# Hybrid trunk on one core: where the input's sums of squares and first modulation tiles are computed, and the order of w_in's blocks

## The chip, the cores and the metric

One core of a Trainium2 chip runs the whole program in one launch. The metric is the device time in microseconds, the median of several runs; a profile shows one execution of the same program. Lines (L255 and the like) are lines of the kernel before.

## The reference, cut

Two layers, 256 tokens, width 2048, all in float32. Each layer mixes the tokens by three groups of heads side by side (four retention heads, eight fox heads, four mLSTM heads), whose inputs are column blocks of one projection w_in:

```python
def reference(x, c, positions, ada_w, ada_b, norm_mix_w, norm_mlp_w, w_in, ...):
    cond = jax.nn.silu(c)
    for layer in range(DEPTH):
        mod = (cond @ ada_w[layer] + ada_b[layer])[:, None, :]
        sh_a, sc_a, g_a, sh_m, sc_m, g_m = jnp.split(mod, N_MOD, axis=-1)
        h = rmsnorm(x, norm_mix_w[layer]) * (1.0 + sc_a) + sh_a
        x = x + g_a * hybrid_mixer(h, positions, w_in[layer], ...)
        h = rmsnorm(x, norm_mlp_w[layer]) * (1.0 + sc_m) + sh_m
        x = x + g_m * (jnp.square(jax.nn.relu(h @ w_ff1[layer])) @ w_ff2[layer])
    return rmsnorm(x, final_norm_w)

def hybrid_mixer(h, ...):
    (rq, rk, rv, rg, fq, fk, fv, ff, mq, mk, mv, mo, mi, mf) = jnp.split(h @ w_in, IN_SPLIT_IDX, axis=-1)
    y_ret = head_norm(retention(rotary(rq), rotary(rk), rv)) * silu(rg)
    y_fox = head_norm(forgetting_attention(fq, fk, fv, ff + fox_f_bias))
    mq, mk = split(silu(causal_conv([mq, mk])))
    y_m = head_norm(mlstm(mq, mk, mv, mi + mlstm_i_bias, mf + mlstm_f_bias)) * sigmoid(mo)
    return (concatenate([y_ret, y_fox, y_m]) * merge_scale) @ w_out
```

## The kernel before

Activations lie transposed (features on partitions): X and the normalised h are 16 k-tiles of 128 features by 256 tokens. Every weight matrix comes in chunks of 512 KB (128x1024, two k-tiles of 512 columns) by SyncE's queue into the pool raw (6 buffers). A chunk is split in two parts for precision: ScalarE rounds it to a high part wh (L224), and VectorE or GpSimd subtracts to the low part wl (L230). Which of the two does it is set by a share per stage, pool_share: the shares are added up and at each whole one the low part goes to GpSimd. TensorE then makes three products per tile (L255 to L257 in form b for q and k blocks, L266 to L268 in form a for v, gate and output blocks), so a chunk is 24 matmuls of 256 columns or 12 of 512. wh and wl have three buffers each.

The modulation vectors are not made by matmuls: the matrix ada_w streams in 512 KB tiles through the pool ada (4 buffers), and VectorE multiplies a tile by the spread condition vector cond (in PSUM) and sums it into one column (L282). `ada_plan` lists the tiles in order, `pump` issues them at a rate per stage, and `mod_fix` folds the finished columns by three small matmuls on TensorE (L292, L293). For the first two k-tiles of layer 0, `ada_first` makes shift and scale by matmuls of one column on TensorE instead (L337), from a copy of these columns in another layout (ada_0).

At the start, ScalarE squares X, VectorE adds the squares up (L391 to L394), two fp32 matmul pairs sum over the partitions (L402) and the reciprocal root is found by Newton steps on 128x2 (`newton`), spread by `stat_spread` and used in `h_make`.

Layer 0 projects w_in in five groups of k-tiles (2, 2, 2, 4, 6), because a group can start as soon as its h is there; each group goes over the first twelve blocks of BLOCKS, and the partial sums are kept in SBUF. The last two blocks follow alone over all k-tiles ("late"). In the last group, the mixers are put to work as soon as their blocks are complete (`mixers`): they are Python generators of which `tick` advances two at a time between the matmuls, so the order of BLOCKS sets the order of retention, mLSTM and fox. Retention and mLSTM need the gate blocks rg and mo before `head_out`, which transposes the normalised heads into the operands of w_out (Y). w_out adds up four chunks kc per output block; the list `order` in `layer` names the groups behind i = 0 to 3 (0 retention, 1 and 2 fox, 3 mLSTM), and the first two output blocks begin with i = 0 and 1. Layer 1 projects all 16 k-tiles in one group, with the first block led (matmuls on X before the root is known).

A scheduler in the compiler orders the instructions of each engine by its own estimate; each engine then runs its queue strictly in that order.

Of the kernel before, what the change touches and what calls it, by code (L numbers as in the profile page):

```python
# [32 lines left out]
BLOCKS = [("rq", 0), ("rk", 512), ("rv", 1024), ("mq", 5128), ("mk", 5640), ("mv", 6152), ("fq0", 2048), ("fk0", 3072),  # L33
          ("fv0", 4096), ("fq1", 2560), ("fk1", 3584), ("fv1", 4608), ("rg", 1536), ("mo", 6664)]
# [13 lines left out]
            pool_win=[1.0, 1.0, 1.0, 1.0, 0.5], pool_late=0.5, pool_out=0.3, pool_ff1=[0.3, 0.8], pool_ff=0.8),  # L48
# [14 lines left out]
class Trunk:  # L63
# [52 lines left out]
    def constants(self):  # L116
# [8 lines left out]
        self.ccol = c.tile([P, KT], F32, name="ccol")  # L125
        nc.sync.dma_start(self.ccol, io["ccol"])
# [9 lines left out]
        nc.scalar.activation(self.ccol, self.ccol, AF.Silu)  # L136
# [134 lines left out]
    def ada(self, l, j, kt):  # L271
# [55 lines left out]
    def ada_first(self, kts):  # L327

        nc = self.nc
        ps = self.bank((P, 512))  # L330
        n = len(kts)
        for i in range(2 * n):
            for h in range(2):
                raw = (self.raw if h else self.adap).tile([P, 8, P], F32, tag="raw" if h else "ada", name=self.name("raw"))
                nc.sync.dma_start(raw, self.io["ada_0"][:, i, 8 * h:8 * h + 8, :])
                for k in range(8):
                    nc.tensor.matmul(ps[:, i:i + 1], lhsT=raw[:, k, :], rhs=self.ccol[:, 8 * h + k:8 * h + k + 1],  # L337
                                     start=i == 0 and h == 0 and k == 0, stop=False, skip_group_check=True)
        for i, j in enumerate((1, 0)):
            s = slice(i * n, i * n + n)  # L340
            nc.tensor.matmul(ps[:, s], lhsT=self.ident, rhs=self.vcol(0, C_ADAB + j * KT + kts[0], n), start=False,
                             stop=True, skip_group_check=True)
        a = self.mod[0]
        nc.vector.scalar_tensor_tensor(a[:, KT + kts[0]:KT + kts[0] + n], ps[:, 0:n], 1.0,
                                       self.vcol(0, C_NMIX + kts[0], n), ALU.add, ALU.mult)
        nc.scalar.copy(a[:, kts[0]:kts[0] + n], ps[:, n:2 * n])
# [684 lines left out]
    def run(self):  # L1031
# [11 lines left out]
        for q in range(4):  # L1043
            self.stat_piece(q)
# [115 lines left out]
```

## Time and profile before

| | us |
|---|---|
| median of 3 runs | 2580.16 (2579.64 to 2580.45) |
| profiled execution | 2578.99 |
| its span, first to last instruction | 2577.0 |
| TensorE busy in the span | 2468.7 (96%) |
| VectorE busy | 1576.0 (61%) |
| ScalarE busy | 1183.5 (46%) |
| GpSimd busy | 732.8 (28%) |

Busy shares are averages over stages with different limits; a busy TensorE may run at the lower of its two clock levels (1.2 and 2.4 GHz), which the column PEclk shows as a share of the higher. Windows are counted from the first instruction.

### The profile page before, as it was taken

What the parts mean: (1) busy time and instruction counts of PE and PEld (TensorE: products, weight loads), DVE (VectorE), ACT (ScalarE), POOL (GpSimd) and SP (SyncE); (2) the same over time, 40 slices, a digit from 0 to 9 for tenths busy, and PEclk for the clock granted to TensorE, in tenths of its full rate; (3) what the DMA queues carried; (4) which work ended last, traced back from release to release, by engine and by line L of the source; (5) the groups of instructions that cost most, each with busy time, mean ns of one, the idle gap of its engine ahead of it and who ended that gap; (6) DMA issues with size and microseconds to landing.
All of it is one profiled execution on the core that took longest, in us unless ns stands there. A gap on an engine that the chain in (4) does not pass through costs nothing.

```text
span 2577.0 us, 46671 instructions
## 1 busy us (share of the span) xinstructions
PE 2468.7 (96%) x19116; PEld 2394.2 (93%) x19116; DVE 1576.0 (61%) x2429; ACT 1183.5 (46%) x1445; POOL 732.8 (28%) x303
## 2 busy tenths in 40 slices
PE   7999998798999999999999899999999999999997
PEld 6899886698999999999998889989999999999997
DVE  3676986589665444444468877656755555554555
ACT  2544453545553444443445454554644444444443
POOL 1786431122576766666661000000000000000000
PEclk9999998899999999999999999999999999999999
DMA  7899876398998887888877677645555555555552
GB/s 276 283 342 327 291 270 224 138 352 318 357 333 319 295 285 277 298 290 288 284 254 255 219 275 269 218 145 180 173 185 184 188 180 188 184 185 183 185 186 101
DMA packets 177390, 630.45 MB, mean 245 GB/s; under 512 B 19732, under 2 KB 24470, under 8 KB 177176
## 3 DMA queue, kind: packets, MB, share of 16 engines
q1 hardware_dynamic: 176744, 627.09, 70.0%
q8 instruction: 149, 2.44, 0.4%
q14 instruction: 65, 0.53, 0.1%
q10 hardware_dynamic: 432, 0.39, 0.1%
HBM read 625.31 MB, written 2.10 MB: 243 GB/s over the span
## 4 chain that ended last, share of the span: by engine, by line
PE 80%; DVE 9%; DMA 3%; issue 3%; POOL 3%; ACT 2%; SPq 0%; DVEq 0%; POOLq 0%; ACTq 0%
PE pj L255 22%; PE pj L256 22%; PE pj L257 22%; PE pj L267 3%; POOL wl L230 3%; PE pj L266 3%; PE pj L268 3%; DVE ada L282 2%; DVE wl L230 2%; DMA ada<-ada_w 2%; PE mx L337 1%; PE mx L625 1%; DMA raw<-w_in 1%; DVE cv L714 1%; ACT wh L224 0%
## 5 line engine op out<-in xcount | busy, mean ns | idle before, releaser
L224 ACT CAST wh<-raw 128x1024 fp32r<-128x1024 f32 x804 | 840.6, 1047 | 1108.6 <-PE pj L257 902.9
L230 DVE TENSOR_TENSOR wl<-raw,wh 128x1024 fp32r<-128x1024 f32 x506 | 622.7, 1232 | 488.4 <-ACT wh L224 487.8
L230 POOL TENSOR_TENSOR wl<-raw,wh 128x1024 fp32r<-128x1024 f32 (+1 forms) x298 | 730.2, 2453 | 635.8 <-ACT wh L224 559.2
L256 PE MATMUL pj<-hh,wl 128*128 128x256 f32 x2912 | 829.9, 285 | 16.6 <-DVE wl L230 16.6
L255 PE MATMUL pj<-hl,wh 128*128 128x256 f32 x2912 | 830.4, 285 | 2.2 <-DVE hl L505 1.4
L257 PE MATMUL pj<-hh,wh 128*128 128x256 f32 x2912 | 828.1, 284 | 0.0
L255 PE MATMUL pj<-blk,wh 128*128 128x256 f32 x2528 | 716.1, 284 | 5.4 <-ACT blk L543 3.0
L256 PE MATMUL pj<-blk,wl 128*128 128x256 f32 x2528 | 715.3, 283 | 5.0 <-DVE wl L230 4.0
L257 PE MATMUL pj<-blk,wh 128*128 128x256 f32 x2528 | 712.7, 282 | 0.0
L282 DVE SCALAR_TENSOR_TENSOR ada<-ada,cond 128x1024 f32<-128x1024 f32 x376 | 453.4, 1215 | 260.5 <-DMA ada<-ada_w 257.8
L256 PEld LDWEIGHTS pj<-hh,wl 128*128 128x128 f32 x2912 | 561.2, 193 | 19.0 <-DVE wl L230 18.2
L255 PEld LDWEIGHTS pj<-hl,wh 128*128 128x128 f32 x2912 | 560.9, 193 | 4.0 <-DVE hl L505 1.9
L257 PEld LDWEIGHTS pj<-hh,wh 128*128 128x128 f32 x2912 | 561.0, 193 | 0.2
L256 PEld LDWEIGHTS pj<-blk,wl 128*128 128x128 f32 x2528 | 481.6, 190 | 5.7 <-DVE wl L230 4.4
L255 PEld LDWEIGHTS pj<-blk,wh 128*128 128x128 f32 x2528 | 480.6, 190 | 6.5 <-ACT blk L543 3.5
L257 PEld LDWEIGHTS pj<-blk,wh 128*128 128x128 f32 x2528 | 480.9, 190 | 0.0
L1054 POOL TENSOR_TENSOR blk<-blk,R 128x1024 f32<-128x1024 f32 x1 | 2.4, 2355 | 1201.8 <-ACT R L424 1201.8
L801 DVE SCALAR_TENSOR_TENSOR X<-pj,mod,X 128x256 f32<-128x256 f32 x284 | 117.8, 477 | 67.4 <-PE pj L257 67.4
L267 PE MATMUL pj<-wl,hh 128*128 128x512 f32 x384 | 152.6, 397 | 3.5 <-DVE wl L230 3.0
L266 PE MATMUL pj<-wh,hl 128*128 128x512 f32 x384 | 151.9, 396 | 0.0
L268 PE MATMUL pj<-wh,hh 128*128 128x512 f32 x384 | 151.0, 393 | 0.0
L267 PEld LDWEIGHTS pj<-wl,hh 128*128 128x128 f32 x384 | 72.3, 188 | 19.4 <-DVE wl L230 5.2
(232 smaller groups left out, 1663.6 us busy)
## 6 DMA issues: line engine op xcount, KB each, us to landing
raw<-w_ff SPq DMA_DIRECT2D x508, 512.0 KB, 4.0
ada<-ada_w SPq DMA_DIRECT2D x376, 512.0 KB, 6.4
raw<-w_in SPq DMA_DIRECT2D x224, 512.0 KB, 5.2
raw<-w_out SPq DMA_DIRECT2D x64, 512.0 KB, 4.5
raw<-ada SPq DMA_DIRECT2D x8, 512.0 KB, 8.7
X<-x SPq DMA_DIRECT2D x4, 512.0 KB, 6.1
raw<-w_ff SPq DMA_DIRECT2D x8, 256.0 KB, 3.5
out<-blk SPq DMA_DIRECT2D x4, 512.0 KB, 2.8
```

What stands on the lines that cost most here:

```text
L224: nc.scalar.copy(hi, raw)
L230: eng.tensor_tensor(lo, raw, hi.bitcast(F32), ALU.subtract)
L255: nc.tensor.matmul(o, lhsT=wh[:, s], rhs=al, start=st, stop=False, skip_group_check=True)
L256: nc.tensor.matmul(o, lhsT=wl[:, s], rhs=ah, start=False, stop=False, skip_group_check=True)
L257: nc.tensor.matmul(o, lhsT=wh[:, s], rhs=ah, start=False, stop=last, skip_group_check=True)
L266: nc.tensor.matmul(o, lhsT=al[:, s], rhs=wh, start=first, stop=False)
L267: nc.tensor.matmul(o, lhsT=ah[:, s], rhs=wl, start=False, stop=False)
L268: nc.tensor.matmul(o, lhsT=ah[:, s], rhs=wh, start=False, stop=last)
L282: nc.vector.scalar_tensor_tensor(raw, raw, 1.0, self.cond, ALU.mult, ALU.mult, accum_out=self.part[l][:, i, h:h + 1])
L337: nc.tensor.matmul(ps[:, i:i + 1], lhsT=raw[:, k, :], rhs=self.ccol[:, 8 * h + k:8 * h + k + 1], start=i == 0 and h == 0 and k == 0, stop= ...
L625: nc.tensor.matmul(ps[:, i * P:i * P + P], lhsT=lt, rhs=v[:, j, c:c + P], start=first, stop=last, skip_group_check=True)
L801: V.scalar_tensor_tensor(self.X(k), ps[:, n * T:n * T + T], self.mod[l][:, c:c + 1], self.X(k), ALU.mult, ALU.add)
```

## The change

The input's sums of squares: `stat_first` lets TensorE multiply the squares by a matrix of ones, 16 fp32 matmuls of 256 columns that add up over the partitions and leave the sum on every partition, so nothing has to be spread; the Newton steps then run on 128x256. The first modulation tiles: `ada_first` and its arrays ada_0 and ccol are gone, the k-tiles 0 and 1 are the first of the plan, and `pump_until` puts their eight tiles on VectorE; the first four of them use buffers of raw. The blocks of w_in: fox first, then mLSTM, then retention, then the gates mo and rg; w_out takes the groups in the order fox, fox, mLSTM, retention. In the last group of layer 0, GpSimd's share of low parts is 0.8 instead of 0.5. The fork of buffers in `newton` makes room in SBUF for the 128x256 tiles.

VectorE at the start, where the reciprocal root and the first modulation tiles are made (nw are Newton's tiles, ada and raw modulation tiles, part their sums). Before:

```order
L375 TENSOR_TENSOR nw_154<-mx_147,nw_154 128x2
L376 SCALAR_TENSOR_TENSOR nw_155<-nw_154,mx_147 128x2
L497 TENSOR_TENSOR mx_258<-X_91,R 128x512
L282 SCALAR_TENSOR_TENSOR ada_351,part_127<-ada_351,cond 128x1024
L282 SCALAR_TENSOR_TENSOR ada_354,part_127<-ada_354,cond 128x1024
```

After:

```order
L355 TENSOR_TENSOR nw_156<-mx_128,nw_155 128x256
L298 SCALAR_TENSOR_TENSOR mod_126<-mx_188,vec 128x2
L283 SCALAR_TENSOR_TENSOR ada_196,part_124<-ada_196,cond 128x1024
L356 TENSOR_TENSOR nw_156<-mx_128,nw_156 128x256
L357 SCALAR_TENSOR_TENSOR mx_128<-nw_156,mx_128 128x256
L355 TENSOR_TENSOR nw_156<-mx_128,nw_155 128x256
L356 TENSOR_TENSOR nw_156<-mx_128,nw_156 128x256
L357 SCALAR_TENSOR_TENSOR mx_128<-nw_156,mx_128 128x256
L355 TENSOR_TENSOR nw_156<-mx_128,nw_155 128x256
L356 TENSOR_TENSOR nw_156<-mx_128,nw_156 128x256
L357 SCALAR_TENSOR_TENSOR nw_157<-nw_156,mx_128 128x256
L492 TENSOR_TENSOR mx_204<-X_91,nw_157 128x512
```

The eight modulation products now stand among the first Newton steps; eight steps of 128x256 follow the last of them (ada_196).

TensorE around group 0 of w_in (pj_450 is its seventh block before, pj_577 its twelfth after; mx_945 and mx_891 are the same mod_fix, for the scale of k-tiles 4 and 5). Before:

```order
L256 MATMUL pj_450<-hh,wl_454 128x256
L257 MATMUL pj_450<-hh,wh_453 128x256
L292 MATMUL mx_945<-part_127,fold 128x2 x2
L293 MATMUL mx_945<-vec,ident 128x2
L255 MATMUL pj_489<-hl,wh_492 128x256
```

After:

```order
L265 MATMUL pj_577<-wh_580,hh 128x512
L293 MATMUL mx_891<-part_124,fold 128x2
L252 MATMUL pj_641<-hl,wh_644 128x256
L293 MATMUL mx_891<-part_124,fold 128x2
L294 MATMUL mx_891<-vec,ident 128x2
L253 MATMUL pj_641<-hh,wl_645 128x256
```

The step moved from the seventh block of group 0 to the first of group 1; the one behind it (the shift) moved from the tenth block of group 0 to behind the second of group 1.

TensorE at the end of the projections of layer 0 (before: pj_4067 is the last gate block, mx_3578 to mx_3684 are fox heads; after: pj_4300 and pj_4454 are w_out's first two output blocks, mx_3969 to mx_4076 retention heads, mx_4125 an output transposition of mLSTM). Before:

```order
L267 MATMUL pj_4067<-wl_4320,hh 128x512
L268 MATMUL pj_4067<-wh_4319,hh 128x512
L665 MATMUL mx_3578<-ident,pt_3587 128x128 x3
L625 MATMUL mx_3578<-blk_546,pt_3587 128x128 x3
L652 MATMUL mx_3684<-blk_520,blk_481 128x128
```

After:

```order
L254 MATMUL pj_4300<-blk_3619,wh_4378 128x256
L620 MATMUL mx_3860<-blk_596,pt_3863 128x128 x3
L609 MATMUL mx_3969<-blk_531,blk_575 128x256
L610 MATMUL mx_3969<-blk_531,blk_575 128x128
L620 MATMUL mx_3969<-blk_596,pt_3972 128x128 x3
L609 MATMUL mx_4015<-blk_531,blk_575 128x256
L610 MATMUL mx_4015<-blk_531,blk_575 128x128
L620 MATMUL mx_4015<-blk_596,pt_4018 128x128 x3
```

Five fox heads stood behind the projections' last matmul and ahead of w_out; now the last three retention heads stand behind w_out's first block, and the mLSTM transposition ahead of its second.

The diff, with the removed function and the loader of its arrays cut:

```diff
-BLOCKS = [("rq", 0), ("rk", 512), ("rv", 1024), ("mq", 5128), ("mk", 5640), ("mv", 6152), ("fq0", 2048), ("fk0", 3072),
-          ("fv0", 4096), ("fq1", 2560), ("fk1", 3584), ("fv1", 4608), ("rg", 1536), ("mo", 6664)]
+BLOCKS = [("fq0", 2048), ("fk0", 3072), ("fv0", 4096), ("fq1", 2560), ("fk1", 3584), ("fv1", 4608),
+          ("mq", 5128), ("mk", 5640), ("mv", 6152), ("rq", 0), ("rk", 512), ("rv", 1024), ("mo", 6664), ("rg", 1536)]
...
-            pool_win=[1.0, 1.0, 1.0, 1.0, 0.5], pool_late=0.5, pool_out=0.3, pool_ff1=[0.3, 0.8], pool_ff=0.8),
+            pool_win=[1.0, 1.0, 1.0, 1.0, 0.8], pool_late=0.5, pool_out=0.3, pool_ff1=[0.3, 0.8], pool_ff=0.8),
...
-        self.ccol = c.tile([P, KT], F32, name="ccol")
-        nc.sync.dma_start(self.ccol, io["ccol"])
...
-        nc.scalar.activation(self.ccol, self.ccol, AF.Silu)
...
-                raw = self.adap.tile([P, n], F32, tag="ada", name=self.name("ada"))
+                early = self.nada < 4
+                self.nada += 1
+                raw = (self.raw.tile([P, n], F32, tag="raw", name=self.name("raw")) if early else
+                       self.adap.tile([P, n], F32, tag="ada", name=self.name("ada")))
...
-    def ada_first(self, kts):
...
+        mk = lambda nm: self.small.tile(list(shape), F32, tag=f"nw{nm}{shape[-1]}", name=self.name("nw"),
+                                          bufs=1 if shape[-1] == T else 2)
...
+    def stat_first(self):
+        nc = self.nc
+        ps = self.bank((P, 512))
+        for q in range(4):
+            sq = self.slot()
+            nc.scalar.activation(sq, self.Xq[q], AF.Square)
+            for i in range(4):
+                nc.tensor.matmul(ps[:, :T], lhsT=self.ones, rhs=sq[:, i, :], start=q == 0 and i == 0,
+                                 stop=q == 3 and i == 3)
+        v = self.small.tile([P, T], F32, name="nv0", bufs=1)
+        nc.vector.tensor_scalar(v, ps[:, :T], 1.0 / D, EPS, ALU.mult, ALU.add)
+        self.R = self.newton(v, (P, T), ps[:, T:2 * T])
...
-        order = [1, 2, 0, 3]
+        order = [1, 2, 3, 0]
...
-        for k in range(2, KT, 2):
+        for k in range(0, KT, 2):
             self.ada_plan([(0, (1, 0), [k, k + 1])])
...
-        self.stat_begin()
-        for q in range(4):
-            self.stat_piece(q)
-        self.stat_end()
-        self.ada_first([0, 1])
-        self.h_make(0, 0, 1, [0, 1], True)
+        self.stat_first()
+        self.pump_until(0, 0, 1)
```

## Rows read from the trace of the kernel before

**Rows 1.** The page, bandwidth in 40 slices of 64.4 us

```profile
GB/s 276 283 342 327 291 270 224 138 352 318 357 333 319 295 285 277 298 290 288 284 254 255 219 275 269 218 145 180 173 185 184 188 180 188 184 185 183 185 186 101
```

**Rows 2.** Stretches of layer 0: busy us (instructions) per engine, granted clock, DMA

```profile
core 0: us, PE busy (x) PEld busy (x) DVE busy (x) ACT busy (x) POOL busy (x), PEclk, DMA share, GB/s
80.00:100.00 20.00, 14.49 (x86) 13.51 (x85) 17.49 (x26) 8.98 (x14) 9.66 (x4) 0.83 0.74 246
100.00:240.00 140.00, 140.00 (x1009) 132.57 (x1008) 101.65 (x135) 60.23 (x72) 112.96 (x47) 1.00 0.94 336
260.00:340.00 80.00, 73.96 (x492) 67.44 (x491) 79.82 (x112) 38.15 (x46) 39.08 (x13) 0.98 0.84 297
423.00:457.00 34.00, 21.58 (x88) 14.94 (x87) 20.38 (x72) 15.20 (x46) 0.00 (x0) 0.64 0.26 99
457.00:500.00 43.00, 29.97 (x203) 27.27 (x204) 21.43 (x61) 23.54 (x46) 4.79 (x2) 0.81 0.21 71
500.00:560.00 60.00, 60.00 (x511) 60.00 (x510) 51.69 (x83) 25.84 (x31) 14.42 (x7) 1.00 0.99 372
```

**Rows 3.** Order of time at the start: start us, duration us, instruction

```profile
4.52 3.78 PE L139 MATMUL cond<-crow,csel 2*128 2x512 f32 x4 [4.52 <-ACT crow L137]
19.25 27.30 PE L337 MATMUL mx<-ccol,raw 128*128 128x1 f32 x128
26.37 1.22 DVE L282 SCALAR_TENSOR_TENSOR ada<-ada,cond 128x1024 f32<-128x1024 f32 x1 [5.77 <-DMA ada<-ada_w]
55.39 0.70 DVE L497 TENSOR_TENSOR mx<-X,R 128x512 f32<-128x512 f32 x1
56.12 0.56 PE L255 MATMUL pj<-hl,wh 128*128 128x256 f32 x1
58.81 0.69 DVE L505 TENSOR_TENSOR hl<-mx,hh 128x512 fp32r<-128x512 f32 x1
60.32 0.41 PE L256 MATMUL pj<-hh,wl 128*128 128x256 f32 x1
60.81 0.28 PE L256 MATMUL pj<-hh,wl 128*128 128x256 f32 x1
```

**Rows 4.** The loads of line 335: issue durations, first and last issue, landing

```profile
L335 SPq DMA_DIRECT2D raw<-ada x8: 328/455/571, 4.5 to 10.9; - x8
DMA to landing us min/median/max: 7.5/8.7/10.2
```

**Rows 5.** Order of time, 80 to 91 us: VectorE, GpSimd and TensorE

```profile
80.24 2.59 DVE L187 TENSOR_SCALAR rt<-rt,rope 128x256 f32<-128x256 f32 x1
80.28 2.40 POOL L230 TENSOR_TENSOR wl<-raw,wh 128x1024 fp32r<-128x1024 f32 x1 [0.43 <-ACT wh L224]
90.54 0.38 PE L292 MATMUL mx<-part,fold 128*128 128x2 f32 x2 [3.18 <-DVE ada L282]
```

**Rows 6.** Groups and single lines, 250 to 424 us (min/median/max ns, or mean ns)

```profile
L230 DVE TENSOR_TENSOR wl<-raw,wh 128x1024 fp32r<-128x1024 f32 x26 | 31.6, 1214 | 5.4 <-ACT wh L224 5.3
L694 DVE TENSOR_TENSOR pt<-mx,decay 128x256 f32<-128x256 f32 x4 | 1.7, 419 | 0.0
L714 DVE SCALAR_TENSOR_TENSOR cv<-blk,vec,cv x24: 460/466/2605, 292.6 to 344.7; 128x255 f32<-128x255 f32 x8, 128x254 f32<-128x254 f32 x8, 128x253 f32<-128x253 f32 x8
L230 POOL TENSOR_TENSOR wl<-raw,wh x26: 2374/2413/5291, 248.6 to 415.6; 128x1024 fp32r<-128x1024 f32 x26
```

**Rows 7.** What TensorE waited for, 423 to 500 us, and its order of time

```profile
PE mx L786 <- ACT blk L771: 11.8, 6, 9.8
471.02 0.94 PE L625 MATMUL mx<-blk,pt 128*128 128x128 f32 x6 [0.21 <-DVE pt L666]
482.86 0.48 PE L786 MATMUL mx<-ident,blk 128*128 128x128 f32 x1 [9.78 <-ACT blk L771]
```

**Rows 8.** Stretches of layer 1, columns as in rows 2

```profile
1420.00:1440.00 20.00, 11.81 (x76) 10.80 (x75) 18.81 (x29) 9.32 (x10) 0.00 (x0) 0.82 0.61 204
1720.00:1740.00 20.00, 16.61 (x110) 15.29 (x110) 7.92 (x18) 11.46 (x20) 0.00 (x0) 0.83 0.30 106
```

More of the change, by code (lines that the diff above doesn't have):

```diff
@@ L325, in flush @@
                 self.h_make(0, 0, 1, kts, True)
-    def ada_first(self, kts):
[L329 to L346, printed above, removed]
     def rate(self, tiles, units):
@@ L365, in newton @@
         n = int(np.prod(shape[1:]))
-        mk = lambda nm: self.small.tile(list(shape), F32, tag=f"nw{nm}{shape[-1]}", name=self.name("nw"))
+        mk = lambda nm: self.small.tile(list(shape), F32, tag=f"nw{nm}{shape[-1]}", name=self.name("nw"),
+                                          bufs=1 if shape[-1] == T else 2)
         y = ps[:, :n] if len(shape) == 2 else ps[:, :n].rearrange("p (a b) -> p a b", b=shape[2])
@@ L1032, in run @@
         nc = self.nc
-        self.pending, self.credit, self.out_tiles, self.U, self.wdma, self.fixes = [], 0.0, [], {}, [], []
-        for k in range(2, KT, 2):
+        self.pending, self.credit, self.out_tiles, self.U, self.wdma, self.fixes, self.nada = [], 0.0, [], {}, [], [], 0
+        for k in range(0, KT, 2):
             self.ada_plan([(0, (1, 0), [k, k + 1])])
@@ L1084, in _layout @@
     a["positions"] = np.ascontiguousarray(inp["positions"][0])
-    a["ccol"] = np.ascontiguousarray(inp["c"].reshape(KT, P).T)
-    w0 = inp["ada_w"][0].reshape(KT, P, 6, KT, P)[:, :, 1::-1, 0:2, :]
-    a["ada_0"] = np.ascontiguousarray(w0.transpose(1, 2, 3, 0, 4)).reshape(P, 4, KT, P)
     a["ada_w"] = np.ascontiguousarray(inp["ada_w"].transpose(0, 2, 1)).reshape(DEPTH, 96, 2, P, D // 2)
```

## The prediction

> **What bounds the kernel now.** I read the bandwidth line of the page first, then a table of stretches (busy time, granted clock, load traffic), then the order of time in the two places where TensorE stands still, and last the VectorE and GpSimd groups of the last w_in group. The projections need TensorE: from 100 to 240 us it is busy 140.00 of 140 us [rows 2]. So a microsecond counts only where TensorE waits or runs at the lower level of its clock. What a stretch loses I take as its length less busy time times granted clock [rows 2]: 80 to 100 us loses 20 - 14.49 x 0.83 = 8.0; 260 to 340 loses 80 - 73.96 x 0.98 = 7.5; 423 to 457 loses 34 - 21.58 x 0.64 = 20.2; 457 to 500 loses 43 - 29.97 x 0.81 = 18.7. In layer 1 the same sum gives 10.3 for 1420 to 1440 and 6.2 for 1720 to 1740 [rows 8]. Ahead of all that, the first projection matmul starts at 56.12 us [rows 3].
>
> **The start.** TensorE makes the first modulation columns itself: 128 one-column matmuls take 27.30 us from 19.25 on [rows 3]. The change removes them, the two spread matmuls and the VectorE sums, and puts 16 fp32 matmuls of 256 columns (sums of squares) on TensorE and eight 128x1024 products on VectorE. The loads are the same in number and size (8 x 512 KB). The pieces:
> - Sums on TensorE: the two 512-column fp32 matmuls of cond take 3.78 us from 4.52 on [rows 3], so one of 256 columns costs 0.95 us at that pace and 0.47 at the doubled pace that matmuls show at 60.81, after TensorE had run since 56.12 without a break (0.41 recorded at 60.32, 0.28 at 60.81) [rows 3]. From 8.3 on, 16 of them end at 15.9 or at 23.4. I take 15.9, since TensorE has work without a break from 4.52.
> - Tiles: the eight loads are issued from 4.5 to 10.9 and land 7.5 to 10.2 us later, so the last is there by about 20 [rows 4]; its product is 1.22 [rows 3]: 21.3.
> - Newton on 128x256 is 13 steps; a VectorE step of that size with a PSUM operand takes 0.419 us [rows 6]. Eight of them stand behind the last product: 3.4, so 24.7. From the multiplication by R to the stored low part is 55.39 to 59.50 = 4.1 us [rows 3]: the first projection matmul at 29. With the sums at 23.4, four products (4.9), 12 steps (5.0) and the 4.1 follow: 37.4. **Term: 56.1 to 29, minus 27 (bounds minus 19 and minus 28).**
>
> **80 to 100 us.** The rope steps on VectorE stand ahead of a modulation product, and TensorE waits 3.18 us for that at 90.54; a rope step of 128x256 takes 2.59 us there, ending with a GpSimd low part that ran beside it [rows 5]. In the new order the mod_fix steps for k-tiles 4 and 5 stand behind group 0 and two blocks into group 1, where before they stood inside group 0. **Term: minus 8, if the products come in time.** They come from the load stream, though: by 240 us it has moved 64.4 x (0.276 + 0.283 + 0.342) + 46.8 x 0.327 = 73.3 MB [rows 1]. The same point would now be due at 240 - 27 - 8 = 205. Ten tiles (5.2 MB) can be ahead of their use, so 68 MB are due by 205, 337 GB/s from the first load on; 100 to 240 us showed 336 with a DMA share of 0.94, and 500 to 560 showed 372 [rows 2]. There is no slack. I take 6 us back (bounds 0 and 20).
>
> **Last w_in group of layer 0 (pool_win 0.5 to 0.8).** 36 chunks: 11 low parts go from VectorE to GpSimd, 11 x 1.214 = 13.4 us less VectorE [rows 6]. VectorE was the bound from 260 to 340 (79.82 of 80) [rows 2]; with fox first, the rotary multiplications leave this place too. Against it: a GpSimd low part has a median of 2.41 us but takes up to 5.29, and the convolution's 24 steps have a median of 0.47 but take up to 2.61 [rows 6]: the two engines hold each other. All 24 held for the longest would be 24 x 2.14 = 51 us; I take four more than now, 9 us, since GpSimd's parts grow from 18 to 29. **Term: minus 4 of the 7.5 lost (bounds minus 7 and plus 12).**
>
> **End of the projections, layer 0.** Before, w_out starts with the fox outputs, which are the last to be computed. TensorE waits 11.8 us for the normalised heads [rows 7]; from the last value product of fox 1 (471.02) to its first output transposition (482.86) it is 11.8 us, 9.78 of it idle [rows 7]. Now fox is done early and w_out's first two blocks cover the rest. What stays: three retention heads in a row behind the projections (scores, two VectorE steps, values), some 2.8 us each with 1.3 of work: 4.5 lost; the mlstm heads' transpositions in front of the second w_out block, with a chain of 11.8 plus its gate (1.2 and the sigmoid's column) less the 9 us of the heads: 5; then the retention's own 13 to 14 us behind some 8 us of matmuls: 5; and 2 at the lower clock. Together 16 of the 38.9. **Term: minus 23 (bounds minus 32 and minus 5).**
>
> **Layer 1.** No group, share or load changes; only the order. Retention's start (rotary on VectorE and ScalarE) meets the gates at 1420, which costs the 10.3; fox's tail costs the 6.2. Fox has no 128x1024 steps at its start, and retention now has two whole blocks behind it. New collisions when the rotary starts beside pool_win 0: 5 of the 16.5 come back. **Term: minus 11 (bounds minus 16 and plus 3).**
>
> **Given back later.** Part of w_out's modulation products and low parts lay in the 77 us in which TensorE was half idle, and now has to run beside full matmuls; from 500 to 560 VectorE is busy 51.69 of 60 and DMA 0.99 [rows 2]. **Term: plus 4 (bounds 0 and plus 15).** The edits to newton's buffers and the w_out order cost nothing by themselves: their price is inside the terms above.
>
> Sum: -27 - 8 + 6 - 4 - 23 - 11 + 4 = -63. The profiled execution takes 2578.99 us (span 2577.0 and 2.0 around it), so 2516; the median of the three runs is 1.2 higher, so **2517 us**.
>
> **Rivals.** (1) *The load stream and VectorE take the gains of layer 0 back.* All layer-0 traffic (to 560 us) is then moved at a pace near what the rows show as an average: the early start and the tail bring the same loads due earlier, and both engines that feed TensorE are at 0.85 to 0.99. Then 20 us are lost up to 240 and 15 in w_out instead of 6 and 4: -38, so **2542**. For it: 336 GB/s with TensorE full. Against it: 372 in 500 to 560, so more is possible. The Trainium skill (SBUF — State Buffer, A bandwidth-pool intuition that's wrong) puts one core's HBM traffic at about 358 GB/s; the 372 of the trace is above that, and the measurement decides. (2) *The tail only changes its name*: mlstm and retention end as late as fox did, because both share two PSUM banks and VectorE with w_out. Then the term is minus 3, and the sum -43: **2537**. (3) *Nothing is given back*: loads and VectorE keep up, the tail loses 8: -27 - 8 - 7 - 31 - 15 = -88, so **2492**. (4) *Slower: GpSimd's low parts become the bound.* A block's chunk takes TensorE some 2.85 us; a low part that VectorE holds takes 5.29 [rows 6]. If all 29 GpSimd parts of the last group take that, TensorE waits 29 x 2.44 = 71 us there, more than the 63 + 4 gained: **2584**. It turns slower from a mean of 5.2 us per part. Against it: the median of 26 is 2.413, so only a few are held, and eleven fewer VectorE low parts hold them. The Trainium skill (SBUF — State Buffer, Who interferes with whom) has it that a VectorE instruction with two SBUF inputs and a GpSimd instruction that reads SBUF shut each other out for a whole instruction; the rope step of 2.59 and the 5.29 agree, and by that rule this case would need every low part to meet such an instruction.
>
> **How the numbers follow.** Forecast as summed 0.46, (1) 0.19, (2) 0.15, (3) 0.16, (4) 0.03, and 0.01 for no difference. The range has to hold eight in ten: the forecast and both middle rivals are in it, with their unknown bounds up to 2555 and, toward (3), down to 2490: **2490 to 2555**. Slower by over 0.2% (about 5 us, what a measurement of this kernel can tell from no change) 0.03, within 0.01, faster 0.96.
>
> **What would show it.** The first projection matmul near 29 us, not 37; no TensorE wait of 3 us on a modulation product before 100; over 330 GB/s up to 210 us; no fox transposition waited for at the end of the projections, but one short wait each for mlstm and retention heads, 16 us lost together; TensorE full where 1420 was, less the time gained. It would be wrong if the first group waits for w_in loads behind the modulation loads, if TensorE waits for GpSimd low parts in the last w_in group, or if w_out of layer 0 waits for weights, which it did not from 500 to 560 [rows 2].

## The result and the profile after

The changed kernel takes **2547.36 us** (median of 4 runs, 2546.65 to 2549.75), against 2579.9 for the kernel before beside it: ratio 0.9877, 95% interval 0.9860 to 0.9894, so 32.5 us faster. The forecast was 2517 with a range of 2490 to 2555: inside the range, with about half of the gain that was summed up. The profiled execution took 2549.75 us (span 2548.0), 29.2 less than the one before. One of the ten runs of the kernel called e8 below took 5384.98 us for no known reason; its median is 2574.05 with it and 2573.85 without. Lines are now those of the changed kernel; L252 to L254, L227, L283 and L293 are what L255 to L257, L230, L282 and L292 were.

The page: busy times, and the bandwidth in 40 slices, to be held against [rows 1].

```profile
PE 2450.1 (96%) x19016; PEld 2378.3 (93%) x19016; DVE 1583.2 (62%) x2427; ACT 1180.9 (46%) x1442; POOL 758.9 (30%) x314
GB/s 359 299 327 329 305 217 265 285 299 338 322 334 310 279 288 297 287 280 298 285 213 241 272 247 266 192 166 178 178 182 186 188 182 183 187 185 183 186 187 91
```

Stretches of the changed kernel (length, busy us of each engine with its instructions, granted clock, DMA share, GB/s), answering to [rows 2] and [rows 8]:

```profile
core 0: us, PE busy (x) PEld busy (x) DVE busy (x) ACT busy (x) POOL busy (x), PEclk, DMA share, GB/s
20.00:40.00 20.00, 11.15 (x61) 10.80 (x62) 14.19 (x27) 7.12 (x10) 8.57 (x4) 0.59 1.02 378
60.00:80.00 20.00, 14.72 (x89) 13.56 (x88) 19.53 (x28) 7.86 (x9) 11.99 (x5) 0.85 0.77 275
100.00:220.00 120.00, 120.00 (x860) 113.38 (x859) 86.33 (x114) 48.78 (x57) 96.36 (x42) 1.00 0.94 332
240.00:320.00 80.00, 80.00 (x572) 74.47 (x571) 70.60 (x136) 37.07 (x62) 47.58 (x20) 1.00 0.87 311
320.00:400.00 80.00, 72.64 (x398) 60.39 (x397) 57.33 (x121) 45.76 (x78) 30.06 (x13) 0.98 0.68 233
400.00:460.00 60.00, 48.24 (x292) 43.00 (x291) 50.36 (x123) 30.05 (x54) 8.78 (x4) 0.83 0.55 199
460.00:520.00 60.00, 60.00 (x511) 60.00 (x510) 48.85 (x78) 26.41 (x32) 14.21 (x7) 1.00 0.96 360
520.00:600.00 80.00, 64.03 (x465) 62.65 (x464) 73.32 (x122) 37.80 (x61) 12.79 (x6) 0.87 0.81 284
1300.00:1360.00 60.00, 49.21 (x352) 48.18 (x352) 42.19 (x69) 31.24 (x53) 21.27 (x9) 0.86 0.58 200
```

Length less busy time times clock, as in the prediction: 60 to 80 us still loses 7.5; 240 to 320 loses nothing (260 to 340 of the kernel before, with VectorE full, lost 7.5); 320 to 400 loses 8.8; 400 to 460 loses 20.0; 520 to 600 loses 24.3; and 1300 to 1360, the joint between the layers, loses 17.7.

What a stretch loses says little where two kernels do different work in it. A second reading does: every variant computes the same projections, so I add up the columns of the pj matmuls in the trace and note when the n-th chunk's worth (6144 columns) is done. Layer 0 has 60 chunks in groups 0 to 3, the last group up to 96, the gate blocks up to 112, w_out up to 144; layer 1 begins at 393. The table gives that time less the time of the kernel before, in us; a step from one row to the next is what the stretch between them won or lost. All columns behind "changed" are the experiments told below (e1, e2, e3, e8, e6, e9, e10 and e12, from left to right); each rests on one execution.

| chunks done | before, at us | changed | start only | order only | share 0.5 | start and share | joint mended | both mends | mends, old start | rope at start |
|---|---|---|---|---|---|---|---|---|---|---|
| 0 | 56.7 | -24.6 | -24.2 | 0.0 | -24.6 | -24.6 | -24.1 | -24.4 | 0.2 | -23.2 |
| 16 | 113.1 | -22.2 | -21.3 | -0.2 | -22.9 | -21.9 | -22.4 | -30.7 | -7.7 | -31.1 |
| 40 | 185.2 | -23.4 | -22.5 | -0.2 | -24.1 | -23.1 | -23.6 | -31.7 | -7.0 | -31.7 |
| 64 | 261.7 | -21.5 | -20.6 | -0.2 | -22.2 | -21.2 | -21.7 | -21.0 | -1.8 | -29.9 |
| 120 | 507.2 | -41.2 | -15.5 | -7.0 | -39.8 | -12.7 | -41.8 | -39.0 | -11.9 | -48.4 |
| 160 | 651.7 | -34.2 | -19.9 | -10.7 | -32.7 | -13.3 | -34.7 | -37.2 | -6.9 | -50.9 |
| 396 | 1329.2 | -33.9 | -20.4 | -11.8 | -33.0 | -13.1 | -31.0 | -35.2 | -4.3 | -48.3 |
| 420 | 1428.9 | -24.5 | -20.2 | -12.7 | -26.7 | -5.3 | -29.4 | -33.7 | -1.1 | -46.6 |
| 516 | 1757.3 | -32.1 | -19.7 | -22.0 | -39.1 | -6.2 | -38.9 | -43.9 | -10.7 | -55.3 |

So the changed kernel's 29.2 us are made up of: start -24.6, groups 0 to 3 +3.1, last group and tail of layer 0 -19.7, w_out and the start of ff1 +7.0, the rest up to chunk 516 +2.1, and +2.9 behind it.

One execution is not exact, and two pairs of columns show by how much. Up to 1290 us, TensorE and VectorE run the same instructions in the same order in the changed kernel and in e6 ("joint mended"); yet e6 is 0.5 us ahead of the changed kernel at chunk 320 and 2.9 behind it at chunk 340, since from 1080 to 1120 us its TensorE is busy 38.27 of 40 us at a granted clock of 0.96, against 40.00 at 1.00. From 1337 us on, the same holds for the changed kernel and e3 ("share 0.5"); yet between chunks 420 and 516 e3 wins 12.4 us and the changed kernel 7.6. So a step of the table can be off by 3 to 5 us.

**The start**, in order of time (start, duration, instruction, idle before):

```profile
7.75 9.53 PE L415 MATMUL mx<-blk,ones 128*128 128x256 f32 x32
22.34 1.21 DVE L283 SCALAR_TENSOR_TENSOR ada<-ada,cond 128x1024 f32<-128x1024 f32 x1
26.69 0.42 DVE L357 SCALAR_TENSOR_TENSOR nw<-nw,mx 128x256 f32<-128x256 f32 x1
31.46 0.58 PE L252 MATMUL pj<-hl,wh 128*128 128x256 f32 x1 [6.84 <-DVE hl L500]
```

**The rope steps**, which make the tables of the rotary embedding, still stand ahead of modulation products, only earlier. 64 to 76 us, VectorE, GpSimd and TensorE:

```profile
65.83 2.44 DVE L196 TENSOR_SCALAR rt<-rt 128x256 f32<-128x256 f32 x1
68.60 2.36 POOL L227 TENSOR_TENSOR wl<-raw,wh 128x1024 fp32r<-128x1024 f32 x1 [0.48 <-ACT wh L221]
68.64 2.59 DVE L201 SCALAR_TENSOR_TENSOR rt<-rt 128x256 f32<-128x256 f32 x1
71.16 1.21 DVE L283 SCALAR_TENSOR_TENSOR ada<-ada,cond 128x1024 f32<-128x1024 f32 x1
72.43 0.38 PE L293 MATMUL mx<-part,fold 128*128 128x2 f32 x2 [3.16 <-DVE ada L283]
```

TensorE waits 3.16 us here, 2.12 once more at 75.16, and then runs at the lower level: the same loss as the wait of 3.18 in [rows 5], moved with the work.

**The joint of the layers**, 1312 to 1323 us:

```profile
1312.30 1.22 DVE L283 SCALAR_TENSOR_TENSOR ada<-ada,cond 128x1024 f32<-128x1024 f32 x1 [1.31 <-DMA ada<-ada_w]
1312.48 7.69 POOL L227 TENSOR_TENSOR wl<-raw,wh 128x1024 fp32r<-128x1024 f32 x3 [1.79 <-ACT wh L221]
1313.44 2.00 DVE L374 TENSOR_TENSOR ss<-ss,blk 128x512 f32<-128x512 f32 x1
1315.36 5.48 DVE L437 SCALAR_TENSOR_TENSOR blk<-X,mod,blk 128x256 fp32r<-128x256 f32 x3
1323.04 1.87 PE L383 MATMUL pj<-ones,ss 128*128 128x1 f32 x8 [6.12 <-DVE ss L375]
```

A modulation product waits 1.31 us for its load, the steps behind it (sum of squares L374, operands of the lead block L437) then run beside three GpSimd low parts, and take 2.0 us, and 5.48 for three, instead of the 0.68 and 0.42 each that they take in e6 below, without those parts. TensorE waits 6.12 us for the second sum of squares (L375) at 1323.04. In the kernel before, both sums stand ahead of that product, and TensorE doesn't wait for them:

```profile
1344.25 0.69 DVE L393 TENSOR_TENSOR ss<-ss,blk 128x512 f32<-128x512 f32 x1
1345.39 0.69 DVE L394 TENSOR_TENSOR ss<-ss,blk 128x512 f32<-128x512 f32 x1
1349.00 1.22 DVE L282 SCALAR_TENSOR_TENSOR ada<-ada,cond 128x1024 f32<-128x1024 f32 x1 [2.13 <-DMA ada<-ada_w]
```

### The profile page after: what moved, and what is told of

The parts are those of the page before. It is cut to its first block, busy times and chain, and to the rows that moved or that the text cites. A ratio compares the mean times of both kernels' runs of the same rounds, so it can differ in the third digit from the quotient of the medians.

```text
span 2548.0 us, 46455 instructions
## 1 busy us (share of the span) xinstructions
PE 2450.1 (96%) x19016; PEld 2378.3 (93%) x19016; DVE 1583.2 (62%) x2427; ACT 1180.9 (46%) x1442; POOL 758.9 (30%) x314
## 3 DMA queue, kind: packets, MB, share of 16 engines
q8 instruction: 149, 2.44, 0.4%
## 4 chain that ended last, share of the span: by engine, by line
PE 79%; DVE 9%; DMA 4%; issue 3%; POOL 3%; ACT 2%; SPq 0%; DVEq 0%; POOLq 0%; ACTq 0%
PE pj L253 23%; PE pj L252 23%; PE pj L254 23%; DMA ada<-ada_w 3%; POOL wl L227 3%; DVE ada L283 2%; PE pj L264 2%; PE pj L265 2%; PE pj L263 2%; DVE wl L227 2%; PE mx L620 1%; ACT wh L221 1%; DVE cv L709 1%; DVE blk L437 0%; DMA raw<-ada_w 0%
## 5 line engine op out<-in xcount | busy, mean ns | idle before, releaser
L227 POOL TENSOR_TENSOR wl<-raw,wh 128x1024 fp32r<-128x1024 f32 (+1 forms) x309 | 756.3, 2451 | 583.4 <-ACT wh L221 565.3
L227 DVE TENSOR_TENSOR wl<-raw,wh 128x1024 fp32r<-128x1024 f32 x495 | 615.7, 1246 | 487.4 <-ACT wh L221 486.7
L252 PE MATMUL pj<-hl,wh 128*128 128x256 f32 x2912 | 830.9, 286 | 9.5 <-DVE hl L500 8.2
L254 PE MATMUL pj<-hh,wh 128*128 128x256 f32 x2912 | 828.1, 284 | 0.0
L252 PE MATMUL pj<-blk,wh 128*128 128x256 f32 x2528 | 712.8, 282 | 2.8 <-ACT blk L538 1.5
L254 PE MATMUL pj<-blk,wh 128*128 128x256 f32 x2528 | 711.3, 281 | 0.0
L283 DVE SCALAR_TENSOR_TENSOR ada<-ada,cond 128x1024 f32<-128x1024 f32 x380 | 456.7, 1214 | 227.7 <-DMA ada<-ada_w 225.6
L252 PEld LDWEIGHTS pj<-hl,wh 128*128 128x128 f32 x2912 | 561.8, 193 | 10.7 <-DVE hl L500 8.9
L254 PEld LDWEIGHTS pj<-hh,wh 128*128 128x128 f32 x2912 | 562.1, 193 | 0.2
L252 PEld LDWEIGHTS pj<-blk,wh 128*128 128x128 f32 x2528 | 478.8, 190 | 3.4 <-ACT blk L538 1.9
L254 PEld LDWEIGHTS pj<-blk,wh 128*128 128x128 f32 x2528 | 479.3, 190 | 0.0
L264 PEld LDWEIGHTS pj<-wl,hh 128*128 128x128 f32 x384 | 73.7, 192 | 24.5 <-DVE wl L227 10.7
```

The source lines that it names most:

```text
L227: eng.tensor_tensor(lo, raw, hi.bitcast(F32), ALU.subtract)
L252: nc.tensor.matmul(o, lhsT=wh[:, s], rhs=al, start=st, stop=False, skip_group_check=True)
L254: nc.tensor.matmul(o, lhsT=wh[:, s], rhs=ah, start=False, stop=last, skip_group_check=True)
L264: nc.tensor.matmul(o, lhsT=ah[:, s], rhs=wl, start=False, stop=False)
L283: nc.vector.scalar_tensor_tensor(raw, raw, 1.0, self.cond, ALU.mult, ALU.mult, accum_out=self.part[l][:, i, h:h + 1])
```

## The experiments

Medians; a ratio is to the kernel before on the same chip in the same sitting. In the five sittings the kernel before took 2576.57 to 2579.9 us, so a difference of medians from two sittings can be off by 2 to 3 us.

| kernel | us | ratio (95% interval) |
|---|---|---|
| changed | 2547.36 | 0.9877 (0.9860 to 0.9894) |
| e1 start only | 2567.65 | 0.9957 (0.9942 to 0.9972) |
| e2 order only | 2557.82 | 0.9928 (0.9909 to 0.9947) |
| e3 changed, share 0.5 | 2547.80 | 0.9882 (0.9864 to 0.9901) |
| e4 changed, layer 1 in the old order | 2552.94 | 0.9909 (0.9892 to 0.9925) |
| e5 changed, constants behind group 2 | 2537.80 | 0.9843 (0.9822 to 0.9864) |
| e6 changed, joint without GpSimd | 2540.03 | 0.9843 (0.9823 to 0.9864) |
| e7 changed, rotary of layer 1 on GpSimd | 2547.46 | 0.9874 (0.9853 to 0.9896) |
| e8 start and share, old order | 2574.05 | 0.9983 (0.9973 to 0.9992) |
| e9 joint mended, constants inside group 3 | 2538.91 | 0.9853 (0.9838 to 0.9867) |
| e10 as e9, old start | 2568.84 | 0.9963 (0.9951 to 0.9975) |
| e11 as e9, w_out share 0.6 | 2539.97 | 0.9855 (0.9840 to 0.9871) |
| **e12 joint mended, rope tables at the start** | **2522.95** | **0.9784 (0.9767 to 0.9801)** |

### The parts alone: e1 and e2

e1 keeps the changed kernel's start and takes back the rest (e2 is the other half: BLOCKS and the w_out order in the kernel before).

```diff
-BLOCKS = [("fq0", 2048), ("fk0", 3072), ("fv0", 4096), ...
+BLOCKS = [("rq", 0), ("rk", 512), ("rv", 1024), ("mq", 5128), ...
-            pool_win=[1.0, 1.0, 1.0, 1.0, 0.8], ...
+            pool_win=[1.0, 1.0, 1.0, 1.0, 0.5], ...
-        order = [1, 2, 3, 0]
+        order = [1, 2, 0, 3]
```

(Lines of e4 and e12 are shifted by one to five against the changed kernel's.)

> The start alone: sums of squares on TensorE and the first modulation tiles on VectorE; blocks, w_out order and share as before. Theory (what the two traces show by matmuls done): the first projection matmul comes 24.6 us earlier, some 3 us of it go to the rope steps, and nothing later takes it back: 2580 - 21 = 2559 us. Rival (the load stream, due earlier, takes part of it back up to the end of layer 0's projections): 2580 - 11 = 2569 us.

> The order alone: w_in's blocks fox, mlstm, retention, mo, rg and w_out's order; old start, share 0.5. Theory: the last w_in group and the tail of layer 0 gain some 20, w_out gives 7 back, layer 1 gives 2 back: 2580 - 11 = 2569 us. Rival (the tail only changes its name, mlstm and retention end as late as fox did): 2580 - 3 = 2577 us.

Measured: the start alone 10.4 us in the median, the order alone 20.2; together 30.6, close to the changed kernel's 32.5. Going from e2 to e3, which differ by the start alone, is 10.0 as well. But the profiled execution of e1 (2559.27) was the quickest of its six (the others 2564.56 to 2569.92), and in its trace the start's 24 us are still 19.7 at chunk 516. So the rival's number was met and its reason not shown: up to chunk 64 nothing but 3.6 us is taken back, and where the other executions lose some 5 to 10 us more, no trace here tells. The order alone gave more than the theory's 11, because layer 1 gains 10.2 with it (-11.8 at chunk 396 to -22.0 at 516): the forecast of -11 for layer 1 fits a kernel whose joint is clean.

### The share: e3 and e8

```diff
-            pool_win=[1.0, 1.0, 1.0, 1.0, 0.8], pool_late=0.5, ...
+            pool_win=[1.0, 1.0, 1.0, 1.0, 0.5], pool_late=0.5, ...
```

That is e3; e8 is e1 with the share left at 0.8.

> The changed kernel with GpSimd's share of 0.5 instead of 0.8 in the last w_in group of layer 0. Theory: eleven low parts return to VectorE (13 us of its time), which is full from 400 to 420 us only, so some 4 us are lost: 2551 us. Rival (the share is worth nothing, or GpSimd holds VectorE): 2543 to 2547 us.

> The changed kernel in the old order of blocks and of w_out: the start and the share 0.8 alone. Theory: with the start alone 10 us are won in the median (2567.65); in the old order VectorE is full from 260 to 340 us, so eleven low parts fewer on it are worth the 7 us lost there: 2561 us. Rival (the share only moves the wait, GpSimd parts being held as long as VectorE's were short): 2567 us.

Both theories fell. In the new order the share is worth nothing (2547.80 and 2547.36); in the old order it costs 6.4 us (2567.65 to 2574.05), 7 us above the rival's 2567. Where these 6.4 go is not shown: e8's trace loses 7.9 us between chunks 64 and 160 where e1's loses 0.7, but also 7.8 at the joint, where e1's loses 0.2. GpSimd itself is not what is late. In the changed kernel its 36 low parts of 230 to 417 us (minimum, median, maximum in ns) are

```profile
L227 POOL TENSOR_TENSOR wl<-raw,wh x36: 2373/2403/3352, 230.7 to 404.5; 128x1024 fp32r<-128x1024 f32 x36
```

against a maximum of 5291 in [rows 6]. e8 also shows that the tail's reading was right: in the old order the fox transposition of [rows 7] is waited for as before, and not in any kernel with the new one.

```profile
471.23 0.47 PE L781 MATMUL mx<-ident,blk 128*128 128x128 f32 x1 [9.83 <-ACT blk L766]
```

### Layer 1: e4 and e7

```diff
+OLD_ORDER = [9, 10, 11, 6, 7, 8, 0, 1, 2, 3, 4, 5, 13, 12]
...
+        if l == 1:
+            b = OLD_ORDER[b]
...
-        order = [1, 2, 3, 0]
+        order = [1, 2, 3, 0] if l == 0 else [1, 2, 0, 3]
```

> The changed kernel with layer 1 alone in the old order (blocks retention, mlstm, fox, rg, mo and w_out retention third). Theory: the new order only exchanges one stall of layer 1 for another, since the rotary of retention meets VectorE low parts wherever it stands: 2545 us, 2 less than the changed kernel, with 10 us lost at the gates again. Rival (the forecast): the order is worth 11 us in layer 1, and something else took them: 2558 us.

Measured 2552.94: neither 2545 nor 2558. The new order is worth 5.6 us in layer 1. With the old one TensorE waits at the gates as it did before (7.7 us there):

```profile
1413.92 0.58 PE L254 MATMUL pj<-hh,wl 128*128 128x256 f32 x1 [8.19 <-DVE wl L228]
```

In the new order the rotary steps of retention meet the low parts later, and for less: VectorE of the changed kernel at 1646, and TensorE's wait.

```profile
1646.28 1.22 DVE L682 TENSOR_TENSOR blk<-blk,blk 128x1024 f32<-128x1024 f32 x1
1647.41 2.35 DVE L227 TENSOR_TENSOR wl<-raw,wh 128x1024 fp32r<-128x1024 f32 x2
1648.69 0.80 PE L264 MATMUL pj<-wl,hh 128*128 128x512 f32 x1 [3.23 <-DVE wl L227]
```

e7 moves these rotary steps to GpSimd, which has no other work in layer 1 behind its first blocks:

```diff
-            V.tensor_tensor(x, x, cb, ALU.mult)
-            V.tensor_tensor(sw, sw, sb, ALU.mult)
-            V.tensor_tensor(x, x, sw, ALU.add)
+            E = nc.gpsimd if l == 1 else V
+            E.tensor_tensor(x, x, cb, ALU.mult)
+            E.tensor_tensor(sw, sw, sb, ALU.mult)
+            E.tensor_tensor(x, x, sw, ALU.add)
```

> The changed kernel with the rotary products of layer 1 on GpSimd, which has nothing else to do there. Theory: at 1641 to 1648 us six 128x1024 rotary steps stand ahead of VectorE's low parts, and TensorE waits 3.2 us and runs at the lower level behind it, 6.9 lost; that is gone: 2541 us. Rival (GpSimd's steps hold VectorE's low parts one by one, as they do in layer 0): 2547 us.

Measured 2547.46, no gain: the rival. Four low parts on VectorE take 12.66 us beside GpSimd's rotary, 3.2 each instead of 1.22, and TensorE waits 2.17 us in place of 3.23:

```profile
1636.38 2.40 POOL L681 TENSOR_TENSOR blk<-blk,cos 128x1024 f32<-128x1024 f32 x1 [298.22 <-ACT blk L679]
1639.54 12.66 DVE L227 TENSOR_TENSOR wl<-raw,wh 128x1024 fp32r<-128x1024 f32 x4 [6.79 <-ACT wh L221]
1642.23 0.69 PE L264 MATMUL pj<-wl,hh 128*128 128x512 f32 x1 [2.17 <-DVE wl L227]
```

### The joint: e6

```diff
                 if nb == 3 and last:
+                    if c == 0:
+                        self.pool_share = 0.0
                     self.early(CFG[l + 1]["early_win"], c, l + 1, 0, 1)
```

> The changed kernel without GpSimd low parts from the last ff2 block of layer 0 to layer 1's blocks (eleven low parts go to VectorE). Theory: at 1308 to 1320 us three GpSimd low parts hold VectorE's steps for the lead block (2.6 us instead of 0.5), which makes the sum of squares 6.1 us late for TensorE; without them that wait is gone: 2541 us. Rival (VectorE needs 13 us more for the eleven low parts, which takes the place): 2547 to 2552 us.

Measured 2540.03, 7.3 less than the changed kernel (8.8 by the ratios), as the theory had it. Between chunks 396 and 420 the changed kernel loses 9.4 us, e6 1.6. The same steps are short again, although VectorE now has eleven low parts more, and TensorE doesn't wait for the sums:

```profile
1310.95 0.68 DVE L374 TENSOR_TENSOR ss<-ss,blk 128x512 f32<-128x512 f32 x1
1311.55 1.27 DVE L437 SCALAR_TENSOR_TENSOR blk<-X,mod,blk 128x256 fp32r<-128x256 f32 x3
1313.28 0.68 DVE L375 TENSOR_TENSOR ss<-ss,blk 128x512 f32<-128x512 f32 x1
```

Who has this loss: the changed kernel, e3, e4, e5, e7 and e8 (6 to 10 us), but not e1 and e2, which have the same GpSimd parts at the joint. It goes with the order of VectorE's instructions there: in e1 and e2, as before, the sums of squares precede the modulation product that waits for a load; in the others one or both follow it. In e6 the sums precede it too, so e6 takes away the GpSimd parts and the turned order at once, and its time alone doesn't tell them apart. The trace does in part: in the changed kernel the load costs 1.31 us there, and the steps that run beside GpSimd parts (a sum of 2.00 us, two operands of 2.61 and 2.56, a cast of 2.03 instead of 0.16) are together some 7 us longer than alone. The change doesn't touch that place; why the compiler's scheduler turned it around was not tried.

### The rope steps and the load stream: e5, e9, e12

e5 makes the late constants behind group 2 (`CONST_AT = 2`), e9 inside group 3, with e6's edit:

```diff
-CONST_AT = 0
+CONST_AT = -1
...
+                if l == 0 and g == 3 and b == 1:
+                    self.late_constants()
...
```

> The changed kernel with the late constants (masks, rope tables) made after group 2 instead of after group 0. Theory: at 70 to 76 us TensorE waits 5.3 us for two modulation products that stand behind rope steps on VectorE, steps that a GpSimd low part holds; without them 7 us are won, and the load stream follows: 2540 us. Rival (loads are the limit up to 240 us, and the products then wait for their tiles): 2547 us, with VectorE waiting for ada_w where it stood in rope steps.

> The changed kernel with the late constants made inside group 3 (behind its second block) and without GpSimd low parts from the last ff2 block of layer 0 on. Theory: the joint is worth 7 us (2540.03 alone), and the rope steps another 8, since the lead of 31 us at chunk 16 is kept when they lie where no modulation product is waited for: 2531 us. Rival (the load stream cannot keep that lead, as it was gone at chunk 48 with the constants behind group 2): 2540 us.

Measured 2537.80 and 2538.91. Both traces show the lead of 31 us at chunk 16, and both show it gone by chunk 48 (-21.4 and -22.7). So e5 came near its theory's 2540 us without its theory's reason, and e9 near its rival's 2540, which foretold the loss but not for its reason. Two stretches of e9:

```profile
80.00:150.00 70.00, 70.00 (x512) 66.54 (x511) 61.08 (x74) 28.32 (x32) 56.81 (x24) 1.00 0.95 333
150.00:190.00 40.00, 34.81 (x219) 32.23 (x219) 34.80 (x48) 13.62 (x18) 25.15 (x11) 0.91 0.81 281
```

and one rope step of the second with the wait that follows:

```profile
158.50 2.23 DVE L201 SCALAR_TENSOR_TENSOR rt<-rt 128x256 f32<-128x256 f32 x1
162.00 0.38 PE L293 MATMUL mx<-part,fold 128*128 128x2 f32 x2 [2.30 <-DVE ada L283]
```

The load stream carries 333 GB/s while TensorE is full, and falls to 281 only where VectorE is late. The rope steps cost about the same wherever they stand beside GpSimd's low parts, which run through all of groups 0 to 3: the changed kernel is 8.5 us behind e9 at chunk 16, e9 loses 9.0 between chunks 40 and 48, and e5 9.8 between 16 and 48. (e5's median is 9.6 us below the changed kernel, more than its profiled run, its slowest, accounts for; that part stays open.) So e12 puts them where GpSimd has nothing: at the very start, with the sine's sign on ScalarE. It has e6's edit too.

```diff
+        self.rt = self.slot()
+        self.rope = c.tile([P, 2], F32, name="rope")
+        nc.scalar.dma_start(self.rt[:, 3, :].bitcast(I32), io["positions"].partition_broadcast(P))
+        nc.scalar.dma_start(self.rope, io["rope"])
...
-        rt = self.raw.tile([P, 4, T], F32, tag="raw", name="rt")
...
-        nc.sync.dma_start(pi.bitcast(I32), self.io["positions"].partition_broadcast(P))
-        rope = c.tile([P, 2], F32, name="rope")
-        nc.sync.dma_start(rope, self.io["rope"])
...
-        V.tensor_scalar(self.sin, self.sin, rope[:, 1:2], None, ALU.mult)
+        nc.scalar.activation(self.sin, self.sin, AF.Copy, scale=rope[:, 1:2])
...
         self.constants()
+        self.rope_tables()
         self.stat_first()
...
```

> The changed kernel with the joint's mend (no GpSimd low parts from the last ff2 block of layer 0 on) and the rope tables made at the very start: their two small loads go first on ScalarE's queue, the VectorE steps stand ahead of the first modulation product, and ScalarE multiplies the sine by its sign. Theory: VectorE waits for loads until 15 us and GpSimd has no low part before 23.7, so nothing holds these steps; the first projection matmul stays at 31.5 us, the 7 to 9 us that the steps cost beside GpSimd's low parts (60 to 80 us in the changed kernel, 143 to 187 us when moved into group 2 or 3) are gone for good, and the lead of 31 us stands at 64 chunks: 2540.03 - 8 = 2532 us. Rival 1 (the load stream cannot feed group 3 at that lead): the lead falls to 22 us by chunk 48 as in both earlier tries, 2540 us. Rival 2 (the steps come too late and delay the products): first matmul at 35 us, 2536 us.

Measured **2522.95**, 17 us less than e6 (15 by the ratios) where 8 were expected, and faster than both kernels. The lead stands at 29.9 at chunk 64 and w_out gives nothing back. The nine rope steps with two operands in SBUF, in the changed kernel and then in e12 (ns: minimum, median, maximum):

```profile
L201 DVE SCALAR_TENSOR_TENSOR rt<-rt x9: 414/424/2593, 68.6 to 79.4; 128x256 f32<-128x256 f32 x9
```

```profile
L202 DVE SCALAR_TENSOR_TENSOR blk<-blk x9: 416/424/426, 7.9 to 12.2; 128x256 f32<-128x256 f32 x9
```

And the stretches of e12 from the first projection matmul on:

```profile
34.00:180.00 146.00, 146.00 (x1042) 138.02 (x1042) 104.28 (x141) 69.88 (x80) 114.47 (x48) 0.99 0.95 341
180.00:260.00 80.00, 79.38 (x591) 75.85 (x590) 62.61 (x99) 33.62 (x40) 55.76 (x24) 1.00 0.94 339
```

TensorE is full for 146 us at 341 GB/s: the load stream feeds it at the whole lead. e12 also frees the raw buffer that the rope tables held and takes their two small loads off SyncE's queue. In the changed kernel these were not what TensorE waited for: from 55 to 95 us its only waits over 1 us are the 5.3 us for VectorE's products, and VectorE never stands idle ahead of any of the 51 products from 60 to 240 us. What e12 gains above the expectation lies between chunks 120 and 160, where e6 gives 7.1 us back and e12 gains 2.5. One of the waits that shrank there is that for a low part in w_out, 1.97 us at 521 where the changed kernel waits 4.57 at 530; what shortens it, and where the rest of these 10 us comes from, was not tried.

### The start once more, and w_out: e10, e11

e10 is e9 with the start of the kernel before, e11 is e9 with `pool_out=0.6` for 0.3.

> The same two mends, order and share 0.8, but the old start (sums of squares on VectorE, modulation columns of k-tiles 0 and 1 on TensorE). It gives the worth of the start alone where the two stalls are gone. Theory (the 24.6 us of the first projection matmul go through, less 3 to 5 in w_out, whose modulation products fall due earlier): 20 us more than the kernel with the new start, 2551 us. Rival (VectorE and the loads take more than half of it back by the end of w_out, as the medians of the start alone suggest, 10 us): 2541 us.

> The two mends and GpSimd's share of low parts in w_out of layer 0 raised from 0.3 to 0.6. Theory: the 7 us that w_out and the start of ff1 give back are VectorE's (from 545 to 592 us it pauses for 0.7 us in all, with modulation products and low parts in its queue), and ten low parts fewer are 12 us less there: 4 us faster than the two mends alone, 2527 us. Rival (GpSimd parts hold VectorE's steps there as at the joint, or the loads set the pace): the same or slower, 2531 to 2537 us.

e10 took 2568.84, so there the start is worth 29.9 us, three times the 10 of e1: its 24.6 go through whole, and e10 meets more waits on the way (one of 5.61 us for a VectorE low part at 434, which e9 does not have). So no single number is right for the worth of the start; that it depends on what else stands in VectorE's queue is likely, but not shown.

e11 took 2539.97, no faster than e9. GpSimd did take the low parts over, but not the wait:

```profile
523.97 4.59 DVE L437 SCALAR_TENSOR_TENSOR blk<-X,mod,blk 128x256 fp32r<-128x256 f32 x6
```

These lead operands (and a modulation product) stand ahead of the low part that TensorE needs at 530.90, and it waits 5.09 us for it. One of the six is held: it takes 2.62 us beside a GpSimd low part of 2.37, where the other five take 0.47 each, which is the rival's first reason. The rest of the wait is the order of the queue and not the sum of VectorE's work, which in 460 to 520 us fell from 47.62 (e9) to 43.77 (e11).

## Why the prediction was right in direction and twice too large

| term | forecast | measured (changed kernel's trace) |
|---|---|---|
| start | -27 (-28 to -19) | -24.6 |
| 80 to 100 us, and the load stream | -8 + 6 | +3.1 |
| last w_in group and tail of layer 0 | -4 - 23 | -19.7 |
| w_out and after | +4 (0 to +15) | +7.0 |
| layer 1 | -11 (-16 to +3) | +2.1 |
| the last block | 0 | +2.9 |

The time lies in the range because the range was wide: two terms, the rope steps and layer 1, missed outright and in the same direction.

**The start** was right to 2.4 us. The step that was off is the end of the last product, put at 21.3. It came at 23.6, since Newton steps stand between the products; the sums ended at 17.3 (forecast 15.9), and the 4.2 us from the multiplication by R to the low part held (forecast 4.1).

**80 to 100 us** failed, and by its own condition. The prediction saw that a GpSimd low part holds the rope steps and that these stand ahead of a product; then it looked at where mod_fix moved and not at whether the rope steps moved with it. They did. The 6 us that the load stream was to take back were not taken: e12 shows 341 GB/s with TensorE full, at a lead of 31 us. "There is no slack" read an average pace (336) as a limit.

**The last group and the tail** were under the forecast by 7. VectorE's relief came (240 to 320 us lose nothing), but the share had little part in it: e3 without it is as fast. The tail keeps more than the 16 us forecast: 400 to 460 alone loses 20.0, about half of it because TensorE runs at the lower clock level for 20.5 us, most of that behind waits of 0.7 to 1.5 us for heads, and 320 to 400 now loses 8.8, where fox heads run inside the projections. So rival 2 was partly right.

**Layer 1** is the largest miss. Its mechanism was right, the gates' wait is gone and e2 gains 10.2 there; by e4 the order is worth 5.6 in the changed kernel. What was missing is the joint: 9.4 us lost between chunks 396 and 420, found in no term, since the prediction took code that the change doesn't touch as unchanged. The compiler had reordered VectorE's instructions there. How large the rest of the miss is stays open: between chunks 420 and 516 the changed kernel wins 7.6 us, e2 9.3 and e3, which runs the changed kernel's instructions there, 12.4.

**The rivals.** Rival 1 was nearest in time (2542) with the wrong engine first: VectorE's queue takes gains back, the load stream doesn't. Rival 4 (GpSimd parts held) is refuted by the 36 parts above. Rival 3's 2492 needs the collisions gone; e12 at 2522.95 goes nearly half of the way there from the changed kernel.

The rope steps, the joint and e7 share one mechanism: a VectorE step with its operands in SBUF that meets a GpSimd instruction can be held for about as long as that one takes. The modulation products of 60 to 240 us, with one operand in PSUM, are not, though GpSimd is busy three quarters of that time:

```profile
L283 DVE SCALAR_TENSOR_TENSOR ada<-ada,cond x51: 1203/1210/1218, 59.6 to 236.3; 128x1024 f32<-128x1024 f32 x51
```

The Trainium skill (SBUF — State Buffer, Who interferes with whom) says just this: a VectorE instruction with two SBUF inputs contends with a GpSimd instruction that reads SBUF, one with a single SBUF input outside the two-port modes does not, and the one that comes later waits for the whole of the other. The traces agree: 0.42 against up to 2.59 us for the same step, and 1.203 to 1.218 for all 51 products. The step of 2.59 us in [rows 5], which the prediction put under two SBUF inputs, has only one tensor input, like L196 at 65.83 (2.44 us): such steps were held as well, and in which mode they ran, no trace shows.

## What to carry to other kernels

Where GpSimd works without a pause, reckon with every short VectorE step on SBUF operands lasting as long as a GpSimd instruction (not all do: the median of the nine rope steps is 0.42 us), and move such steps to a time when GpSimd has nothing; moving them within its busy time moves the loss along. A term that ends "if the steps in front are gone" has to be followed in the order of the instructions, also at places that the change doesn't touch, because a scheduler may have turned them around. The gain of one part isn't a number of its own: the same start was worth 10 and 30 us beside different neighbours.

## What the runs showed of the hardware that was not expected

The same wait can cost different amounts. At the last output block TensorE waits 1.91 us (changed) and 1.90 us (before) for the same sum, after 15 us in which it was busy without a break at the higher level (2500 to 2515 and 2532 to 2547); in the one execution the clock then falls to the lower level, in the other it does not. 15 us of the changed kernel and the same 15 of the kernel before:

```profile
2515.00:2530.00 15.00, 11.94 (x71) 11.31 (x70) 4.54 (x7) 4.94 (x11) 0.00 (x0) 0.77 0.00 0
```

```profile
2547.00:2562.00 15.00, 11.95 (x98) 11.32 (x96) 4.61 (x7) 5.56 (x12) 0.00 (x0) 1.00 0.00 0
```

The granted clock is 0.77 here and 1.00 there, which accounts for the 2.9 us behind chunk 516 that no part of the change explains (6.8 us at half speed are 3.4). It goes with differences between executions of one kernel, too: e2 took 2552.84 us at a mean granted clock of 0.985 and 2564.01 at 0.981, and 0.004 of the span is 10 us. But it is not all of them: e1 took 2559.27 and 2568.68 us with a mean of 0.976 both times. So one profile is not enough to price a part of this size. And the load stream, taken as full at 336 GB/s, moved 378 from 20 to 40 us.
